# A decoder trunk on one core: all SBUF operands at one address modulo 256, another order of the first chunks, and a position read requested one unit earlier

## The chip, the cores and the metric

The kernel runs on one core of a Trainium2 chip. The metric is the device time of one execution in microseconds, shown as the median of several runs. Lower is better. A profiled execution has its own time and a span, which is the time from its first to its last instruction. TensorE is called PE below (PEld is its load of the stationary operand), VectorE is DVE, ScalarE is ACT, GpSimd is POOL, and SyncE is SP.

## The reference

One layer works on 1024 positions of 1024 float32 values each. In short:

```python
hn = rms_norm(h)
proj = hn @ w_in                                   # 1024 x 10256: u, v, lru, ssd, dt and gate columns
ya = u * (tril(w_s) @ layer_norm(gelu(v)) + b_s)   # position mixing in chunks of 128, 8 groups
yb = gelu(gate) * linear_scan(conv(xb))            # RG-LRU, 8 heads
yc = ssd(conv(xbc), dt, z)                         # Mamba-2 chunked scan, 4 groups
h = h + (sum_k sigmoid(g_k) * (y_k @ w_branch_k)) @ w_out
h = h + relu(rms_norm(h) @ w_up) ** 2 @ w_down
out = rms_norm(h)
```

The large products are made in three fp32r passes each (high times high, high times low, low times high), so every float32 operand is first split into a high and a low part: ACT writes the high part and DVE or POOL the difference. The two products of the last block use Strassen's seven products on half matrices.

## The kernel before

The code is one function, `trunk_kernel`. Its stages follow each other in this order:

- **The first chunks** (0 to about 58 us, lines 283 to 419), written out by hand, each engine in program order. The eight row chunks of `x` (128 positions each) are squared and summed on ACT (`row_sum`, line 319), their reciprocal root is made by `row_root` (line 322: for row 0 wholly on DVE, for the others three DVE and twelve POOL operations), they are scaled (`row_scale`, lines 325 to 328: on DVE or, with `True`, on POOL), transposed on PE (`transpose_rows`, line 159) and split (`x_high` on ACT, `x_low` on DVE). `v_start` makes the first block of v from them, 24 matmuls for each chunk. 18 matmuls of `ones` by `ones` (line 338, `WARM`) run first, while the first loads are under way. The norm's gains come from the DMA of line 294 through a transpose (line 344) and a copy to `g2c` (line 345).
- **Constants** (lines 421 to 453): transposes of the position weights `wT` (line 443), and the row sums of `wT` by a float32 matmul with `ones` (line 450), which feed `bs`. From here on a planner puts the instructions in order by priority; matmuls wait in PE's program order.
- **The other blocks of v** (`v_block`), with a layer norm of v whose result is written to DRAM as `vn_d` (line 825).
- **Units** (`run`, line 494): each unit is a product of 48 matmuls (line 492, `ps <- w . X`) with a `post` that takes its result. Three units' weights are prepared ahead. After each unit, `step` advances every generator in `pending` by one `yield`. `dt_stages` (line 526) is such a generator: softplus and `adt` in the first step, then, one unit later, matmuls with `tri` and `ones` (lines 534 and 535). `gmlp_unit` (line 765) is another: its first step requests the group's slice of `vn_d` on POOL's queue (line 768), the second, one unit later, multiplies it by `wT` (line 774).
- **The branches** (the second `run`): the same product, with the mixers' outputs `Y` in place of `X`; then `w_out` (line 917).
- **Up and down** (line 948, `seventh`), and the last norm (lines 1364 to 1425), whose reciprocal roots are in tiles `rs0` to `rs7`.

**Where operands lie.** Pools are stacked in SBUF in the order in which they are opened; `xn` and `act3` are taken from the other end. A tile of the small pool takes at least 32 bytes. The allocation of this kernel, in bytes of each partition:

| pool | names in the profile | first address | tile, bytes | address modulo 256 |
|---|---|---|---|---|
| base | ident, g2c, vh | 16512 | | 128, 128, 224 |
| w | wh, wl, wb, wt | 17632 | 4096 | 224 |
| raw | raw, rt | 42208 | 4096 | 224 |
| small | rsq, rs, fs, ... | 50400 | | |
| half | h | 51808 | 2048 | 96 |
| act | a | 84576 | 4096 | 96 |
| act2, opened where half was | a | 51808 | 4096 | 96 |
| lru | lr, lw | 146016 | 1024 | 96 |
| const | bs, wT, ones, tri, ... | 149088 | | bs, wT, ones: 0 |
| xn and act3 | xn, b | 163808 | 4096 | 224 |

Slices of these tiles that are operands of fp32r matmuls begin at multiples of 512 bytes from the tile's start, so an operand has its pool's residue. Right after the small pool come the pools half, act and const, whose start its size sets. The small pool begins with a tile that nothing uses:

```python
    sm(8, "spacer")
```

Of the kernel before, what the change touches and what calls it, by code (L numbers as in the profile page):

```python
# [9 lines left out]
F32R = mybir.dt.float32r  # L10
# [6 lines left out]
P = 128  # L17
# [10 lines left out]
C_U, C_V, C_XB, C_GATE, C_Z, C_XBC, C_DT, C_G = 0, 1024, 2048, 3072, 4096, 5120, 7168, 7184  # L28

VBLOCKS = ((678, 346, False), (0, 340, True), (340, 338, False))  # L30
WARM = 18
AHEAD = 2

# [2 lines left out]
def trunk_kernel(ctx: ExitStack, tc: tile.TileContext, x, norm_mix_g, w_in, b_gate, gmlp_ln_g, gmlp_ln_b,  # L36
# [42 lines left out]
    def sm(n, tag, dt=F32, bufs=None):  # L79
        return small.tile([P, n], dt, tag=tag, name=nm(tag), bufs=bufs)  # L80

    sm(8, "spacer")

    tt = nc.vector.tensor_tensor
    stt = nc.vector.scalar_tensor_tensor
# [197 lines left out]
    with tc.manual_schedule():  # L283

        rows, v_ps, xt = [], [None] * NCH, [None] * NCH

        def row_load(c):
            rows.append(act())
            nc.sync.dma_start(out=rows[c], in_=x[c * P:(c + 1) * P, :])

        g_rows = act()[:16, :P]
        row_load(0)
        for i, g in enumerate((norm_mix_g, norm_mlp_g)):
            nc.scalar.dma_start(out=g_rows[8 * i:8 * i + 8, :], in_=g[0].rearrange("(n p) -> n p", p=P))
        v_raw[0][0] = v_load(0, 0, rawp)
        row_load(1)
        v_raw[0][1] = v_load(0, 1, rawp)
        for i in (2, 3):
            v_raw[0][i] = v_load(0, i, None)
        for c in range(2, NCH):  # L300
            row_load(c)

        ident = base.tile([P, P], F32, name="ident")
        make_identity(nc, ident)
        ones = const.tile([P, P], F32, name="ones")
        nc.vector.memset(ones, 1.0)
        tri = const.tile([P, P], F32, name="tri")
        nc.gpsimd.affine_select(out=tri, in_=ones, pattern=[[1, P]], compare_op=ALU.is_ge, fill=0.0,
                                base=0, channel_multiplier=-1)
        neg = const.tile([P, P], F32, name="neg")  # L310
        ts(out=neg, in0=tri, scalar1=-1.0, scalar2=3.0e38, op0=ALU.add, op1=ALU.mult)
        g2c = base.tile([P, 2 * KD], F32, name="g2c")
        eps4 = base.tile([P, 1], F32, name="eps4")
        nc.vector.memset(eps4, 4.0 * EPS)
        ss, rs = sm(NCH, "ss"), sm(NCH, "rsx")
        v2[NCH - 1] = act()

        def row_sum(c):
            actv(v2[NCH - 1], rows[c], AF.Square, accum_out=ss[:, c:c + 1])

        def row_root(a, b):
            (rsqrt_cols if a else rsqrt_col)(rs[:, a:b], ss[:, a:b], 1.0 / D, EPS)

        def row_scale(c, pool=False):
            if pool:
                nc.gpsimd.tensor_scalar(out=rows[c], in0=rows[c], scalar1=rs[:, c:c + 1], scalar2=0.0, op0=ALU.mult, op1=ALU.add)
            else:
                ts(out=rows[c], in0=rows[c], scalar1=rs[:, c:c + 1], scalar2=None, op0=ALU.mult)

        def v_start(c, ks):  # L330
            if ks[0] == 0:
                v_ps[c] = aux()
            v_matmuls(0, wv0, c, v_ps[c], ks)


        ps = aux()
        for i in range(WARM):
            mm(ps[:, :P], ones, ones, start=True, stop=True)
        row_sum(0)
        row_root(0, 1)  # L340
        row_scale(0)
        wv0 = v_weights(0, (0,), nc.gpsimd)
        ps = aux()
        nc.tensor.transpose(out=ps[:, :16], in_=g_rows[:16, :], identity=ident[:16, :16])
        actv(g2c, ps[:, :16], AF.Copy)
        xt[0] = transpose_rows(rows[0])
        row_sum(1)
        row_root(1, 2)
        wv0 += v_weights(0, (1,))
        x_high(xt[0], 0, 0)  # L350
        x_low(xt[0], 0, 0)
        x_high(xt[0], 0, 1)
        row_scale(1)
        x_low(xt[0], 0, 1)
        v_start(0, range(0, 4))
        xt[1] = transpose_rows(rows[1])
        wv0 += v_weights(0, (2,), nc.gpsimd, nc.vector)
        wv0 += v_weights(0, (3,), None, nc.vector)
        v_start(0, range(4, 8))
        row_sum(2)  # L360
        row_root(2, 3)
        for q in range(2):
            x_high(xt[1], 1, q)
            x_low(xt[1], 1, q)
        row_scale(2)
        row_sum(3)
        row_sum(4)
        row_root(3, 5)
        row_scale(3, True)
        row_scale(4, True)  # L370

        for i in range(2):
            v_raw[1][i] = v_load(1, i, rawp)
        nc.sync.dma_start(out=dtb, in_=ssd_dt_bias[0].partition_broadcast(P))
        load_rows(acs, [b_gate.rearrange("k (n p) -> (k n) p", p=P), rows_of(gmlp_ln_g[0]), rows_of(gmlp_ln_b[0]),
                        rows_of(lru_conv_b[0]), rows_of(lru_b_r[0]), rows_of(lru_b_i[0]), rows_of(lru_lambda[0]),
                        rows_of(ssd_norm_g[0]), rows_of(ssd_conv_b[0]),
                        lru_conv_w[0].rearrange("k (n p) -> (k n) p", p=P)])
        load_rows(nacs, [ssd_conv_w[0].rearrange("k (n p) -> (k n) p", p=P)])
        nc.sync.dma_start(out=wT, in_=gmlp_w_s[0].rearrange("g t s -> t g s"))  # L380
        nc.sync.dma_start(out=bs, in_=gmlp_b_s[0].partition_broadcast(P))
        nc.sync.dma_start(out=al, in_=ssd_a_log[0].partition_broadcast(P))
        v_start(1, range(0, 4))
        xt[2] = transpose_rows(rows[2])
        v_start(1, range(4, 8))
        wv1 = []
        for c in range(1, NCH):

            if c > 1:
                if c + 1 < NCH:  # L390
                    xt[c + 1] = transpose_rows(rows[c + 1])
                v_start(c, range(0, 8))
            sq = gelu_in(c - 1)
            if c + 1 < NCH:
                x_high(xt[c + 1], c + 1, 0)
                x_low(xt[c + 1], c + 1, 0)
            if v2[c - 1] is None:
                v2[c - 1] = act()
            gelu_out(c - 1, sq)
            if c + 1 < NCH:  # L400
                x_high(xt[c + 1], c + 1, 1)
                x_low(xt[c + 1], c + 1, 1)
            if c in (1, 2):
                for i in ((5,), (6, 7))[c - 1]:
                    row_sum(i)
            if c == 2:
                row_root(5, 8)
                for i in (5, 6, 7):
                    row_scale(i, True)
            if c == 4:  # L410
                nc.gpsimd.affine_select(out=wT, in_=wT, pattern=[[0, 8], [-1, P]], compare_op=ALU.is_ge, fill=0.0,
                                        base=0, channel_multiplier=1)
                nc.gpsimd.tensor_scalar(out=bs, in0=bs, scalar1=0.5, scalar2=0.0, op0=ALU.mult, op1=ALU.add)
                for h in range(2):
                    nc.sync.dma_start(out=dcol[64 * h:64 * h + 64, :], in_=ssd_d[0].rearrange("(t h) -> h t", h=2)[h].partition_broadcast(64))
            if c >= 4:
                wv1 += v_weights(1, (c - 4,), nc.gpsimd)
        gelu_out(NCH - 1, gelu_in(NCH - 1))
# [22 lines left out]
    wps = [aux() for _ in range(2)]  # L441
    for i in range(8):
        nc.tensor.transpose(out=wps[i // 4][:, i % 4 * P:(i % 4 + 1) * P], in_=wT[:, i, :], identity=ident)
    for q in range(2):
        actv(wT[:, q * 4:q * 4 + 4, :], wps[q].rearrange("p (c n) -> p c n", c=4), AF.Copy)


    for q in range(2):
        ps = aux()
        mm(ps, ones, wT[:, q * 4:q * 4 + 4, :].rearrange("p c n -> p (c n)"), start=True, stop=True)  # L450
        for i in range(4):
            g = q * 4 + i
            stt(out=bs[:, g, :], in0=ps[:, i * P:(i + 1) * P], scalar=vh[:, LNB + g:LNB + g + 1], in1=bs[:, g, :], op0=ALU.mult, op1=ALU.add)
# [72 lines left out]
    def dt_stages():  # L526
        softplus(dt.rearrange("p c h -> p (c h)"), dtr.rearrange("p c h -> p (c h)"))
        tc.keep_in_program_order(actv(na, al, AF.Exp))
        ts(out=adt, in0=dt, scalar1=-1.0, scalar2=None, op0=ALU.mult)
        tt(out=adt, in0=adt, in1=na.unsqueeze(1).to_broadcast([P, NCH, 16]), op=ALU.mult)  # L530
        yield
        adt_f = adt.rearrange("p c h -> p (c h)")
        ps_a = aux()
# [175 lines left out]
    def lru_units(h):  # L709
# [16 lines left out]
        def post_g(ps):  # L726
            S["g2"] = act()
            gelu2(S["g2"], ps, T)
            later(stages())

        def stages():
            xb, w = S["xb"], S["w"]
# [29 lines left out]
        unit_in(C_GATE + h * P, post_g)  # L762


    def gmlp_unit(g):
        def stages(u2):
            vg = act((P, NCH, P))
            nc.gpsimd.dma_start(out=vg, in_=vn_d[:, g * P:(g + 1) * P].rearrange("(c p) d -> p c d", p=P))
            yield
            y = act()  # L770
            for half in range(2):
                ps = aux()
# [7 lines left out]
        def post(ps):  # L780
            u2 = act()
            gelu2(u2, ps, T)
            later(stages(u2))

        unit_in(C_U + g * P, post)

# [438 lines left out]
    with tc.manual_schedule():  # L1225
# [126 lines left out]
        for c in (4, 5, 6, 7, 0, 1, 2, 3):  # L1352
            H[c] = act()
            nc.scalar.dma_start(out=H[c], in_=h_d[c])
            if c == 7:
                dn_product(0, 0)
                prev.p4()
                prev.last_sum()
        sums, scaled = {}, {}

        def out_row(c, nb, o):
            nc.sync.dma_start(out=out[c * P:(c + 1) * P, hsl(nb)], in_=o)

        def row_scale(c):
            rs = sm(1, f"rs{c}")
            tt(out=sums[c, 0], in0=sums[c, 0], in1=sums[c, 1], op=ALU.add)
            rsqrt_col(rs, sums[c, 0], 1.0 / D, EPS)
            return rs
# [75 lines left out]
```

## Time and profile before

| | us |
|---|---|
| median of 3 runs | 2046.13 (2044.41 to 2046.42) |
| the profiled execution | 2047.5 |
| its span | 2045.8 |
| PE busy | 2001.9 (98%) |
| DVE busy | 1197.6 (59%) |
| ACT busy | 786.3 (38%) |
| POOL busy | 349.8 (17%) |
| mean granted PE clock | 0.993 of full |

In the groups and the timeline a row names a line of the kernel, an engine, the tiles (out<-in, with the moving and the stationary operand for a matmul), and the count. A busy matmul is longer than the distance to the next one, because matmuls are pipelined; what counts is the distance from start to start. Times in a timeline are from the start of the span, and what stands in brackets is the idle time of the engine before the row and what ended it.

### The profile page before, as it was taken

How to read it: one execution, taken by the hardware profiler on the slowest of the kernel's cores; microseconds unless marked ns; L12 is line 12 of the kernel's file. 1: busy time of each engine (PE TensorE's matmuls, PEld its weight loads, DVE VectorE, ACT ScalarE, POOL GpSimd, SP SyncE). 2: the span in 40 equal slices, each digit the busy share in tenths (PEclk: the TensorE clock that was granted, in tenths of full speed). 3: DMA queues.
4: the chain of work that ended last, by engine and by line, in shares of the span. 5: the costliest groups of instructions: out<-in, count | busy, mean ns of one | idle time of the engine just before them, and what ended most of it. 6: DMA issues, size and time to landing. Idle time of an engine off the chain costs nothing.

```text
span 2045.8 us, 23749 instructions
## 1 busy us (share of the span) xinstructions
PE 2001.9 (98%) x9300; PEld 1658.2 (81%) x9300; DVE 1197.6 (59%) x1822; ACT 786.3 (38%) x1076; POOL 349.8 (17%) x374
## 2 busy tenths in 40 slices
PE   8999999999999999999999999999899999999996
PEld 7988888888888888888888888887788887888885
DVE  6596864784585668431122224336756557787687
ACT  6422542353244325322221111146555555243243
POOL 5102232223124113332000320000111110000000
PEclk9999999999999999999999999999999999999998
DMA  4324233423333323343333442421443448544532
GB/s 155 81 108 88 76 95 82 97 72 95 74 85 100 75 78 93 113 124 114 103 103 109 147 125 83 155 82 63 165 160 125 168 149 300 189 135 133 185 105 92
DMA packets 202213, 239.39 MB, mean 117 GB/s; under 512 B 11140, under 2 KB 148564, under 8 KB 202100
## 3 DMA queue, kind: packets, MB, share of 16 engines
q1 hardware_dynamic: 175636, 144.91, 24.0%
q0 software_dynamic: 21680, 75.64, 11.3%
q10 hardware_dynamic: 4784, 17.31, 2.4%
q8 instruction: 73, 1.20, 0.2%
q14 instruction: 40, 0.33, 0.1%
HBM read 174.78 MB, written 63.05 MB: 116 GB/s over the span
## 4 chain that ended last, share of the span: by engine, by line
PE 83%; DVE 8%; ACT 4%; issue 2%; POOL 2%; DMA 1%; ACTq 0%; POOLq 0%; DVEq 0%
PE ps L492 47%; PE aux L948 26%; PE aux L917 4%; PE aux L255 2%; PE aux L740 1%; PE aux L774 1%; DVE rsq_q L109 1%; PE aux L639 1%; PE aux L659 1%; ACT a L977 1%; PE aux L663 1%; DVE bst L819 0%; PE aux L677 0%; ACT a L130 0%; DVE b L131 0%
## 5 line engine op out<-in xcount | busy, mean ns | idle before, releaser
L492 PE MATMUL ps<-xn,wh 128*128 128x512 f32 x2304 | 625.1, 392 | 0.0
L492 PEld LDWEIGHTS ps<-xn,wh 128*128 128x128 f32 x2304 | 431.0, 188 | 93.1 <-issue 4.2
L492 PE MATMUL ps<-xn,wl 128*128 128x512 f32 x1152 | 354.9, 389 | 0.0
L130 ACT ACTIVATE wh<-raw 128x1024 fp32r<-128x1024 f32 x96 | 101.7, 1059 | 402.9 <-PE ps L492 327.1
L492 PEld LDWEIGHTS ps<-xn,wl 128*128 128x128 f32 x1152 | 216.3, 188 | 45.5
L948 PE MATMUL aux<-a,b 128*128 128x512 f32 x864 | 203.0, 395 | 0.0
L948 PEld LDWEIGHTS aux<-a,b 128*128 128x128 f32 x864 | 162.2, 188 | 39.2
L131 DVE TENSOR_TENSOR wl<-raw,wh 128x1024 fp32r<-128x1024 f32 x64 | 81.4, 1272 | 180.7 <-ACT wh L130 180.5
L131 POOL TENSOR_TENSOR wl<-raw,wh 128x1024 fp32r<-128x1024 f32 x32 | 76.8, 2400 | 557.2 <-ACT wh L130 530.6
L948 PE MATMUL aux<-b,wt 128*128 128x512 f32 x672 | 157.2, 389 | 0.0
L948 PEld LDWEIGHTS aux<-b,wt 128*128 128x128 f32 x672 | 126.2, 188 | 26.6
L492 PE MATMUL ps<-a,wh 128*128 128x512 f32 x512 | 140.3, 395 | 0.0
L492 PEld LDWEIGHTS ps<-a,wh 128*128 128x128 f32 x512 | 96.1, 188 | 23.3
L948 PE MATMUL aux<-b,b 128*128 128x512 f32 x480 | 110.8, 389 | 0.0
L1197 DVE TENSOR_TENSOR a<-aux,a 128x512 f32<-128x512 f32 x112 | 77.0, 688 | 55.8 <-PE aux L948 55.7
L948 PEld LDWEIGHTS aux<-b,b 128*128 128x128 f32 x480 | 90.1, 188 | 19.0
L130 ACT ACTIVATE b<-wt 128x1024 fp32r<-128x1024 f32 x60 | 61.8, 1053 | 73.3 <-DMA wt<-u_d 61.5
L948 PE MATMUL aux<-a,wt 128*128 128x512 f32 x336 | 82.3, 401 | 3.3 <-ACT a L1074 3.3
L492 PE MATMUL ps<-a,wl 128*128 128x512 f32 x256 | 80.6, 395 | 0.0
L948 PEld LDWEIGHTS aux<-a,wt 128*128 128x128 f32 x336 | 64.1, 191 | 19.4 <-ACT a L1074 4.2
L512 DVE SCALAR_TENSOR_TENSOR a<-ps,scw,a 128x1023 f32<-128x1023 f32 (+2 forms) x48 | 61.4, 1280 | 25.6 <-ACT a L510 24.5
L1049 POOL DMA_DIRECT2D u_d<-a x48 | 34.5, 720 | 228.6 <-DVE a L1097 177.5
(292 smaller groups left out, 2951.5 us busy)
## 6 DMA issues: line engine op xcount, KB each, us to landing
raw<-in_w_in_dram SPq DMA_DIRECT2D x72, 512.0 KB
wt<-u_d SPq DMA_DIRECT2D x54, 512.0 KB
u_d<-a POOLq DMA_DIRECT2D x48, 512.0 KB, 4.9
rt<-in_w_mlp_up_dram SPq DMA_DIRECT2D x17, 512.0 KB
a<-acs_d POOLq DMA_DIRECT2D x32, 256.0 KB, 6.9
g_d<-a POOLq DMA_DIRECT2D x16, 512.0 KB, 5.2
a<-g_d ACTq DMA_DIRECT2D x16, 512.0 KB
a<-in_w_mlp_down_dram SPq DMA_DIRECT2D x16, 512.0 KB
```

What stands on the lines that cost most here:

```text
L109: stt(out=q, in0=r, scalar=nh, in1=r, op0=ALU.mult, op1=ALU.mult)
L130: actv(dst_hi, src, AF.Copy)
L131: (eng or nc.vector).tensor_tensor(out=dst_lo, in0=src, in1=dst_hi.bitcast(F32), op=ALU.subtract)
L255: mm(ps[:, :nt], X.tok(a, k, c), wk[k][w], start=(k == 0 and i == 0), stop=(k == KD - 1 and i == 2))
L492: mm(ps[:, hsl(h)], w[wi][:, k, :], a.rhs(ai, k, h), start=(n == 0), stop=(n == 3 * KD - 1))
L512: stt(out=dst[:, j:], in0=ps[:, :T - j], scalar=taps[3 - j], in1=dst[:, j:], op0=ALU.mult, op1=ALU.add)
L639: mm(st[:, cc * 256:cc * 256 + 256], Bt[:, 2 * q + cc, :], xw[q][:, cc].rearrange("p h d -> p (h d)"), start=True, stop=True)
L659: mm(yo[:, tok(i)], pv[c // 2][:, c % 2, j * P:(j + 1) * P], Cf[:, tok(c)], start=True, stop=True)
L917: mm(ps, M.tok(a, k, c), wo[nb][k][w], start=(k == 0 and a + w == 0), stop=(k == KD - 1 and a == 1))
L948: mm(ps, lhs[l][kk], rhs[r][kk], start=(new and n == 0), stop=(n == 11), skip_group_check=not new)
L1049: nc.gpsimd.dma_start(out=u_d[i:i + 2, self.s].rearrange("f p t -> p f t"), in_=t.rearrange("p (f t) -> p f t", f=2))
L1197: tt(out=h, in0=ps, in1=h, op=ALU.add)
```

## The change

- The unused first tile of the small pool grows from 8 to 32 floats (96 bytes more), and the eight tiles `rs0` to `rs7` (32 bytes each) become columns of one tile `roots` (32 bytes), 224 less. The pool gets 128 bytes smaller, and every pool after it moves down by 128: half, act, act2 and lru from residue 96 to 224, const from 0 to 128.
- In the first chunks the transpose to `g2c` is put between the ninth and the tenth warm-up matmul, and its copy ahead of `row_sum(0)` on ACT. The high part of the third weight pair is made by ACT in place of DVE. The root of row 2 alone and that of rows 3 and 4 become one root of rows 2 to 4; sums of rows 5 to 7 are spread differently.
- The row sums of `wT` are made by two fp32r matmuls on a split copy, in place of a float32 matmul.
- `dt_stages` waits one unit more before its matmuls.
- The slice of `vn_d` for group g+1 is requested in the `post` of group g, that for group 0 in the `post` of the last RG-LRU gate.

```diff
+SPACER = 32
-    sm(8, "spacer")
+    sm(SPACER, "spacer")
...
-        ps = aux()
+        ps, gps = aux(), aux()
         for i in range(WARM):
+            if i == WARM // 2:
+                nc.tensor.transpose(out=gps[:, :16], in_=g_rows[:16, :], identity=ident[:16, :16])
             mm(ps[:, :P], ones, ones, start=True, stop=True)
+        actv(g2c, gps[:, :16], AF.Copy)
         row_sum(0)
         row_root(0, 1)
         row_scale(0)
         wv0 = v_weights(0, (0,), nc.gpsimd)
-        ps = aux()
-        nc.tensor.transpose(out=ps[:, :16], in_=g_rows[:16, :], identity=ident[:16, :16])
-        actv(g2c, ps[:, :16], AF.Copy)
         xt[0] = transpose_rows(rows[0])
...
-        wv0 += v_weights(0, (2,), nc.gpsimd, nc.vector)
+        wv0 += v_weights(0, (2,), nc.gpsimd)
         wv0 += v_weights(0, (3,), None, nc.vector)
         v_start(0, range(4, 8))
         row_sum(2)
-        row_root(2, 3)
-        for q in range(2):
-            x_high(xt[1], 1, q)
-            x_low(xt[1], 1, q)
-        row_scale(2)
+        x_high(xt[1], 1, 0)
+        x_high(xt[1], 1, 1)
         row_sum(3)
         row_sum(4)
-        row_root(3, 5)
+        x_low(xt[1], 1, 0)
+        row_root(2, 5)
+        x_low(xt[1], 1, 1)
+        row_scale(2)
         row_scale(3, True)
         row_scale(4, True)
+        row_sum(5)
...
             if c in (1, 2):
-                for i in ((5,), (6, 7))[c - 1]:
-                    row_sum(i)
+                row_sum(c + 5)
...
+    wsum, one_r = [act((P, 2, HF), F32R) for _ in range(2)], act(dt=F32R)[:, :P]
+    actv(one_r, ones, AF.Copy)
     for q in range(2):
+        split(wsum[q][:, 0], wsum[q][:, 1], wps[q])
         actv(wT[:, q * 4:q * 4 + 4, :], wps[q].rearrange("p (c n) -> p c n", c=4), AF.Copy)
...
-        mm(ps, ones, wT[:, q * 4:q * 4 + 4, :].rearrange("p c n -> p (c n)"), start=True, stop=True)
+        for i in range(2):
+            mm(ps, one_r, wsum[q][:, i], start=(i == 0), stop=(i == 1))
...
         tt(out=adt, in0=adt, in1=na.unsqueeze(1).to_broadcast([P, NCH, 16]), op=ALU.mult)
+        yield
         yield
...
             later(stages())
+            if h == 7:
+                v_group(0)
...
+    v_of = {}
+
+    def v_group(g):
+        if g < 8:
+            v_of[g] = act((P, NCH, P))
+            nc.gpsimd.dma_start(out=v_of[g], in_=vn_d[:, g * P:(g + 1) * P].rearrange("(c p) d -> p c d", p=P))
+
     def gmlp_unit(g):
         def stages(u2):
-            vg = act((P, NCH, P))
-            nc.gpsimd.dma_start(out=vg, in_=vn_d[:, g * P:(g + 1) * P].rearrange("(c p) d -> p c d", p=P))
             yield
+            vg = v_of.pop(g)
...
             later(stages(u2))
+            v_group(g + 1)
...
+        roots = sm(NCH, "roots")
...
-            rs = sm(1, f"rs{c}")
+            rs = roots[:, c:c + 1]
```

## The prediction

> **What bounds the kernel now.** I read the page's busy times first, then who waited for whom on PE.
>
> ```profile
> PE 2001.9 (98%) x9300; PEld 1658.2 (81%) x9300; DVE 1197.6 (59%) x1822; ACT 786.3 (38%) x1076; POOL 349.8 (17%) x374
> ...
> PE rps L159 <- POOL a L326: 3.2, 2, 2.1
> PE rps L159 <- DVE a L328: 3.0, 3, 1.2
> PE aux L774 <- DMA a<-vn_d: 2.4, 1, 2.4
> PE aux L534 <- DVE adt L530: 0.9, 1, 0.9
> ```
>
> The columns of the waits are total, times and longest, in us. PE is busy for 98% of the span and has few waits, so time is gained where the distance between two matmuls shrinks or where one of these waits goes. The distance is read from PE's timeline, from one row's start to the next, divided by the count.
>
> ```profile
> 1025.74 1.07 PE L492 MATMUL ps<-xn,wh 128*128 128x512 f32 x4
> 1027.10 1.09 PE L492 MATMUL ps<-a,wh 128*128 128x512 f32 x4
> 1028.49 1.10 PE L492 MATMUL ps<-a,wh 128*128 128x512 f32 x4
> 1504.92 2.89 PE L948 MATMUL aux<-a,a 128*128 128x512 f32 x12
> 1507.65 8.33 PE L948 MATMUL aux<-b,wt 128*128 128x512 f32 x36
> 1796.12 22.55 PE L948 MATMUL aux<-a,b 128*128 128x512 f32 x96
> 1818.51 11.06 PE L948 MATMUL aux<-b,b 128*128 128x512 f32 x48
> 1829.41 0.86 PE L948 MATMUL aux<-a,b 128*128 128x512 f32 x3
> ```
>
> All are fp32r matmuls of 512 columns at the full clock. From 1796.12 to 1818.51 lie 96 matmuls of a with b: 22.39 / 96 = 233.2 ns each. The 48 of b with b take 10.90 / 48 = 227.1; the 12 of a with a take 2.73 / 12 = 227.5. The six from 1025.74 (four with wh, two with wl, xn moving) take 1.36 / 6 = 226.7; the six from 1027.10, with a moving, 1.39 / 6 = 231.7. By the table of addresses a lies at residue 96, and b, xn, wh, wl and wt at 224. So pairs of one residue take 227, whether both are at 96 or both at 224; pairs of different residues take about 6 ns more. Neither the engine load around them nor the tile's own address sorts the rows like that.
>
> **The change part by part.**
>
> **Addresses.** The small pool loses 128 bytes, and a goes from 96 to 96 - 128 = 224 modulo 256. These are the groups whose residues differ now and will be equal, by line and form:
>
> ```profile
> L948 PE MATMUL aux<-a,b 128*128 128x512 f32 x864 | 203.0, 395 | 0.0
> L492 PE MATMUL ps<-a,wh 128*128 128x512 f32 x512 | 140.3, 395 | 0.0
> L948 PE MATMUL aux<-a,wt 128*128 128x512 f32 x336 | 82.3, 401 | 3.3 <-ACT a L1074 3.3
> L492 PE MATMUL ps<-a,wl 128*128 128x512 f32 x256 | 80.6, 395 | 0.0
> L917 PE MATMUL aux<-a,b 128*128 128x512 f32 x240 | 59.5, 401 | 0.0
> L1219 PE MATMUL aux<-a,wt 128*128 128x512 f32 x48 | 13.2, 438 | 2.0 <-ACT a L130 1.2 <-DVE a L131 0.8
> L948 PE MATMUL aux<-b,a 128*128 128x512 f32 x48 | 11.6, 396 | 0.0
> ```
>
> Their count is 864 + 512 + 336 + 256 + 240 + 48 + 48 = 2304. At 233.2 - 227.1 = 6.1 ns that is 14.1 us. Not all reaches the end. The last two groups (96 matmuls, 0.6) lie ahead of the wait of line 1219, where ACT and DVE are late. And from here on DVE sets the end:
>
> ```profile
> 2010.03 0.69 DVE L1197 TENSOR_TENSOR a<-aux,a 128x512 f32<-128x512 f32 x1 [2.11 <-PE aux L948]
> ```
>
> This is DVE's last idle before the norm's tail. The block of 96 a with b that is then running ends at 2018.23, so 8.2 / 0.233 = 35 matmuls (0.2 us) come too late to help. I take 14.1 - 0.8 = 13.3. The bounds are 0 (the residue is not the cause) and 14.1. The small tile roots brings no wait: DVE writes one column per row, and ACT's reads of the column before it have ended in the tail by then.
>
> The v blocks are narrower, and there h with xn and a with xn differ now:
>
> ```profile
> 65.78 3.04 PE L255 MATMUL aux<-wb,xn 128*128 128x356 f32 x18
> 68.66 1.13 PE L255 MATMUL aux<-a,xn 128*128 128x356 f32 x6
> 99.78 19.53 PE L255 MATMUL aux<-h,xn 128*128 128x338 f32 x121
> ```
>
> With 356 columns an equal pair takes 2.88 / 18 = 160.0 and an unequal one (1.13 - 0.32) / 5 = 162, the last matmul's 0.32 left off. With 338 columns the unequal ones take (19.53 - 0.32) / 120 = 160; what an equal one takes no row shows: at least 160 - 18 * 227 / 512 = 152, if it goes by columns. There are 8 chunks * 24 = 192 of 346, 192 of 338 and 48 of 356 columns, 432 in all. The bounds are 0 and 432 * 8 = 3.5 us; by the nearest row, 1.7 ns or so, I take 0.7.
>
> [...]
>
> **Position values.**
>
> ```profile
> 830.79 1.80 POOL L768 DMA_DIRECT2D a<-vn_d  x2
> 836.70 3.58 PE L774 MATMUL aux<-wT,a 128*128 128x128 f32 x16 [2.42 <-DMA a<-vn_d]
> 836.60:840.00 3.40, 3.31 (x15) 3.34 (x16) 2.28 (x3) 1.06 (x1) 0.00 (x0) 0.50 0.62 176
> ```
>
> The last is a row of the view by windows; 0.50 is the granted clock. The first request on POOL stands at 830.79, behind the last RG-LRU head's work, and two slices are requested together; PE waits 2.42 for the first. In the change it is issued in the post of the last gate, ahead of that head's work, a unit (48 * 0.227 + stages, 12 us) earlier; 836.7 - 830.8 = 5.9 us are needed. The next slice stays behind the head's work, at about 830, but is needed a unit later. So the wait goes: 2.4. After it the clock was halved for 3.40 us, so 1.7 us of work were lost; no idle, no halving: 1.7 more. Sum 4.1, bounds 0 (the request is held by another wait) and 4.1. The extra tile of a is taken when the last SSD group has released its own.
>
> [...]
>
> **Dt.** The matmul of line 534 waits 0.9 for softplus; a unit later, after 12 us, adt is long there, and its readers start two units on. Gain 0.9, bounds 0 and 1.0.
>
> **First chunks.**
>
> ```profile
> 1.12 7.13 PE L338 MATMUL aux<-ones 128*128 128x128 f32 x36 [1.12 <-DVE ones L306]
> 4.51 1.06 ACT L319 ACTIVATE a<-a 128x1024 f32<-128x1024 f32 x1 [1.49 <-DMA a<-in_x_dram]
> 8.45 0.18 ACT L345 ACTIVATE g2c<-aux 128x16 f32<-128x16 f32 x1 [1.37 <-PE aux L344]
> 19.07 0.15 DVE L116 TENSOR_SCALAR rsqn_r<-ss 128x1 f32<-128x1 f32 x1
> 19.64 0.18 ACT L319 ACTIVATION_READ_ACCUMULATOR a<-a 128x1 f32 x1
> 22.96 0.75 DVE L328 TENSOR_SCALAR a<-a,rsx 128x1024 f32<-128x1024 f32 x1 [1.30 <-POOL rsx L124]
> 23.77 1.09 PE L159 MATMUL rps<-ident,a 128*128 128x128 f32 x8 [0.84 <-DVE a L328]
> 28.85 1.09 PE L159 MATMUL rps<-ident,a 128*128 128x128 f32 x8 [2.08 <-POOL a L326]
> 39.59 1.09 PE L159 MATMUL rps<-ident,a 128*128 128x128 f32 x8 [1.13 <-POOL a L326]
> ```
>
> The transpose to g2c comes at half of the warm-up, 1.12 + 7.13 / 2 = 4.7; ACT's copy follows at about 5.0 and ends at 5.2. It stands ahead of row_sum(0), which started at 4.51, so row 0's chain starts 0.7 later. ACT's high part in place of DVE's frees POOL's low part earlier and takes a short PE stall away, but then one root for rows 2 to 4 waits for the sums of rows 3 and 4: these ended at 19.82, now 0.7 later at 20.5. The root and the scaling take 23.71 - 19.07 = 4.6, so row 2's transposes go from 23.77 to about 25.3, with PE idle for some 4 us and the clock likely halved after it. In return rows 3 and 4 are scaled at once: row 3's transposes come when row 2's chunk is through, 3.0 later, at 28.3 to 29.5 instead of 28.85. Before row 5's root one sum fewer (1.06 + 0.19) stands on ACT, which covers the 1.13 at 39.59. I take a gain of 0.5 in all. Bounds: gain 4.8 (the waits of 0.84, 2.08 and 1.13 all go, with 0.7 of halved clock), loss 2 (the 0.7, and 1.3 of clock and late transposes).
>
> **Row sums of wT.**
>
> ```profile
> 60.11 1.98 PE L450 MATMUL aux<-wT,ones 128*128 128x512 f32 x4
> 61.52 3.45 PE L255 MATMUL aux<-wb,xn 128*128 128x356 f32 x18
> ```
>
> Four fp32r matmuls at 227 are 0.9 in place of 61.52 - 60.11 = 1.4. But they wait for a split, on DVE 0.69 for 512 columns as in line 1197, twice, and ACT has two more copies. I take a loss of 0.3, bounds gain 0.5 and loss 1.5.
>
> **Sum.** 13.3 + 0.7 + 4.1 + 0.9 + 0.5 - 0.3 = 19.2. The profiled execution took 2047.5, so 2028.3; it lies 1.4 above the median of 2046.13, against which the forecast is 2027.
>
> **The rivals.**
>
> - *Addresses do nothing.* What sorts the rows would be something else that goes with them, and 14.0 of the sum fall away: 2046.1 - 5.2 = 2041. Against it stand rows of 227 in one stage and for one line with rows of 233.
> - *The gain is eaten in the last product.* DVE is nearest its limit there, and PE would wait for split operands. From 1796 to 2010 and in the block before it lie most of the 864 a with b; if all of these gain nothing, 864 * 6.1 = 5.3 are lost: 2032. Against it: PE has no wait in that stage and DVE idles 2.11 at its end.
> - *The request stays late.* If the slot for slice 0, or POOL's queue, holds it, 4.1 stay: 2031.
> - *Slower: one address for all.* When everything shares a residue, ACT's, DVE's and POOL's accesses to a meet PE's reads of xn and wh, and no pair is fast. Its place is the units:
>
> ```profile
> L492 PE MATMUL ps<-xn,wh 128*128 128x512 f32 x2304 | 625.1, 392 | 0.0
> L492 PE MATMUL ps<-xn,wl 128*128 128x512 f32 x1152 | 354.9, 389 | 0.0
> ```
>
> If these 3456 take 6.1 more and the 2304 stay at 233, the time is 2041 + 21 = 2062. It decides from 5.1 / 3456 = 1.5 ns on. Against it: a with a, where DVE works on a too, and b with b take 227.
>
> **How the numbers follow.** Forecast 76%, addresses nothing 8%, eaten 7%, request late 5%, slower 4%. What a measurement tells from no change is 0.2%, 4.1 us: below 2042.0 is faster. Forecast, eaten, late and most of the second case lie below it: 0.93; no change 0.03; slower 0.04. The forecast's own range takes the narrow v blocks (2.8 better), the first chunks (4.3 better, 2.5 worse), the wT sums (0.8 better, 1.2 worse) and one clock halving more or fewer (1.7): 2019 to 2033. With the two rivals beside it I give 2018 to 2036.
>
> **What would show it.** Rows of a with b and a with wh at 227; no wait on vn_d, no 0.50 near 836; no wait at line 534; row 2's transposes later, rows 3 and 5 without a wait. Rows at 233 with equal residues would make it wrong.

## The result and the profile after

| | before | after |
|---|---|---|
| median, us | 2046.22 (2044.41 to 2046.51) | 2031.64 (2030.49 to 2033.04) |
| the profiled execution | 2047.5 | 2033.04 |
| its span | 2045.8 | 2031.3 |
| mean granted PE clock | 0.993 | 0.991 |

After over before is 0.9931, with a 95% interval of 0.9918 to 0.9944: 14.6 us faster. The forecast was 2027, so the change gained 4.6 less than forecast, while the time lies within the range.

The first lines are from the page of the kernel after: its busy times, and, from its groups by line and form, three that the prediction listed (busy time, mean ns of one). Lines have moved: the unit product is now line 497, `seventh` line 963, the last subtraction line 1212.

```profile
PE 1985.2 (98%) x9300; PEld 1658.2 (82%) x9300; DVE 1196.5 (59%) x1819; ACT 788.4 (39%) x1081; POOL 348.7 (17%) x362
...
L963 PE MATMUL aux<-a,b 128*128 128x512 f32 x864 | 197.3, 389 | 0.0
...
L497 PE MATMUL ps<-a,wh 128*128 128x512 f32 x512 | 136.8, 389 | 0.0
...
L963 PE MATMUL aux<-a,wt 128*128 128x512 f32 x336 | 80.3, 396 | 3.4 <-ACT a L1089 3.4
```

PE has the same 9300 matmuls and is 16.7 us less busy. Each of these three groups, whose residues became equal, lost 5 to 6 ns in the mean (395 to 389, 395 to 389, 401 to 396). The distance from start to start says the same, in PE's timeline of the kernel after:

```profile
1785.48 21.92 PE L963 MATMUL aux<-a,b 128*128 128x512 f32 x96
1807.24 11.04 PE L963 MATMUL aux<-b,b 128*128 128x512 f32 x48
1818.12 12.18 PE L963 MATMUL aux<-a,b 128*128 128x512 f32 x53
```

96 of a with b take 21.76 us, 226.7 ns each, where they took 233.2; the 48 of b with b take 10.88 / 48 = 226.7. Six with a moving (four with wh, two with wl) take 1.36 from 1025.97 on, 226.7 each, where they took 1.39 before.

To see where the rest went, I compare when the same matmul starts in the two traces:

| from, to | before, us | after, us | gained (+) or lost (-) |
|---|---|---|---|
| start of the span to the last matmul of the first v block | 57.34 | 58.56 | -1.2 |
| to the first of the second v block | 4.18 | 5.46 | -1.3 |
| to the last of the second v block | 31.07 | 32.49 | -1.4 |
| to the first unit | 30.87 | 30.86 | 0.0 |
| first unit to the 53rd | 662.82 | 662.27 | +0.6 |
| to the 61st (position values requested) | 104.61 | 100.27 | +4.3 |
| to the first of w_out (branches) | 402.45 | 397.18 | +5.3 |
| to the first of up and down | 110.65 | 109.79 | +0.9 |
| to the last matmul | 624.91 | 616.85 | +8.1 |
| to the end of the span | 16.89 | 17.60 | -0.7 |

The last three stages of matmuls (5.3, 0.9 and 8.1) hold the addresses' gain. The request gained 4.3. The start lost 3.9, where the prediction had a gain of 0.9 (chunks 0.5, narrow v blocks 0.7, row sums -0.3). The waits of PE after, and its clock in three windows, show the start (columns of the windows: length, busy times of PE, PEld, DVE, ACT and POOL, granted clock, DMA share, GB/s):

```profile
PE rps L160 <- DVE a L329: 6.2, 2, 4.8
...
PE rps L160 <- DVE rsqn_r L117: 2.5, 1, 2.5
...
PE aux L455 <- ACT a L131: 1.2, 1, 1.2
...
PE aux L549 <- DVE w L546: 1.0, 1, 1.0
...
23.90:30.70 6.80, 4.30 (x17) 4.30 (x18) 3.14 (x9) 3.14 (x10) 3.94 (x8) 0.50 0.54 160
64.80:68.20 3.40, 3.40 (x14) 3.40 (x13) 3.40 (x18) 0.53 (x2) 0.00 (x0) 0.51 0.00 0
836.60:840.00 3.40, 3.40 (x25) 3.11 (x24) 1.68 (x2) 1.97 (x2) 0.00 (x0) 1.00 0.91 228
```

The waits on vn_d and on adt are gone from the list. New in it are a wait of 2.5 for row 0 (1.22 before), one of 4.8 for row 2 and one of 1.2 for the split of the wT sums, and the wait for adt came back at line 549 as one for `w` of line 546. The clock is no longer halved at 836.6 (1.00, before 0.50), but it is from 23.9 on for 6.8 us (0.50; before, one stretch of 3.4 at 0.50 from 17.4 on) and at 64.8 (0.51), where the kernel before had full clock (1.00).

### The profile page after: what moved, and what is told of

It is laid out like the page before. It is cut to its first block, busy times and chain, and to the rows that moved or that the text cites. A ratio compares the mean times of both kernels' runs of the same rounds, so it can differ in the third digit from the quotient of the medians.

```text
span 2031.3 us, 23733 instructions
## 1 busy us (share of the span) xinstructions
PE 1985.2 (98%) x9300; PEld 1658.2 (82%) x9300; DVE 1196.5 (59%) x1819; ACT 788.4 (39%) x1081; POOL 348.7 (17%) x362
## 4 chain that ended last, share of the span: by engine, by line
PE 87%; DVE 5%; ACT 4%; issue 2%; POOL 1%; ACTq 0%; POOLq 0%; DVEq 0%
PE ps L497 49%; PE aux L963 26%; PE aux L256 4%; PE aux L932 3%; PE aux L748 1%; ACT a L992 1%; PE aux L788 1%; PE aux L645 1%; DVE rsq_q L110 1%; PE aux L665 1%; PE aux L669 1%; PE aux L683 0%; ACT a L131 0%; DVE b L132 0%; ACT a L970 0%
## 5 line engine op out<-in xcount | busy, mean ns | idle before, releaser
L963 PE MATMUL aux<-a,b 128*128 128x512 f32 x864 | 197.3, 389 | 0.0
```

Of the source, the lines that this page charges most:

```text
L963: mm(ps, lhs[l][kk], rhs[r][kk], start=(new and n == 0), stop=(n == 11), skip_group_check=not new)
```

## The experiments

The theory after the result: equal residues give 14 us and the request gives 4; the chunks, the wT sums and dt give nothing or lose. The rivals, tested against it: that something else than the residue makes the matmuls faster; that only the distance of 128 is slow; that the start's losses are one loss, in the chunks.

### Addresses alone

```diff
 (on the kernel before)
-    sm(8, "spacer")
+    sm(32, "spacer")
...
+        roots = sm(NCH, "roots")
...
-            rs = sm(1, f"rs{c}")
+            rs = roots[:, c:c + 1]
```

> The kernel before with the change of addresses alone: the unused first tile grows to 32 floats and the eight one-column tiles become columns of one tile, so that a lies at residue 224. The theory (the residue of a matmul's two operands sets the distance to the next) expects all fp32r matmuls of 512 columns at 227 ns and 13.3 us less than before, about 2033 us, with the waits on vn_d and at the dt matmul still there. The rival (what sorts the rows is something else) expects 233 ns for a with b as before and about 2046 us.

Measured: 2031.36 (2029.8 to 2033.41), ratio 0.9932 (0.992 to 0.9944), 14.3 us under the kernel before. PE's waits and timeline:

```profile
PE aux L774 <- DMA a<-vn_d: 2.2, 1, 2.2
...
1784.54 21.92 PE L948 MATMUL aux<-a,b 128*128 128x512 f32 x96
1806.30 11.04 PE L948 MATMUL aux<-b,b 128*128 128x512 f32 x48
```

The wait on vn_d is still there, and a with b takes 21.76 / 96 = 226.7. So the 128 bytes alone are worth what the whole change is worth. The remaining four parts together are worth nothing that these runs can tell.

### Other residues

```diff
 (on the kernel after, three kernels)
-SPACER = 32
+SPACER = 64     # a at 96, distance 128
+SPACER = 16     # a at 160, distance 64
+SPACER = 24     # a at 192, distance 32
```

> The changed kernel with an unused tile of 64 floats, so that a is back at residue 96, a distance of 128 from w and b, and all else is as changed. The theory expects 233 ns for a with b and a with wh, 227 for the rest, and 13 us more than the changed kernel, about 2045 us. The rival expects the changed kernel's 2031.6 us.

> The changed kernel with an unused tile of 16 floats: a at residue 160, a distance of 64 from w and b. No theory of mine has a sharp number for this distance: if any difference costs the same, 233 ns and about 2045 us; if the cost goes with the distance, about 230 ns and 2038 us; if only a distance of 128 costs, 227 ns and 2031.6 us.

> The changed kernel with an unused tile of 24 floats: a at residue 192, a distance of 32 from w and b. If any difference costs the same, 233 ns and about 2045 us; if the cost goes with the distance, about 228.5 ns and 2035 us; if only a distance of 128 costs, 227 ns and 2031.6 us.

Measured: 2047.67 (2045.8 to 2049.11), 2048.19 (2046.51 to 2050.02) and 2048.33 (2047.51 to 2049.73); ratios 1.001 (1.0001 to 1.0019), 1.0013 (1.0004 to 1.0022) and 1.0014 (1.0005 to 1.0023). PE's timeline for distance 64, then for distance 32:

```profile
1797.37 22.56 PE L963 MATMUL aux<-a,b 128*128 128x512 f32 x96
1819.77 10.61 PE L963 MATMUL aux<-b,b 128*128 128x512 f32 x46
```

```profile
1796.86 22.56 PE L963 MATMUL aux<-a,b 128*128 128x512 f32 x96
1819.27 11.07 PE L963 MATMUL aux<-b,b 128*128 128x512 f32 x48
```

22.40 / 96 = 233.3 and 22.41 / 96 = 233.4. At distance 128 the 96 take 22.39 from 1797.26 on, 233.2 each. At these three distances the price is the same; of these kernels only those with equal residues have a with b at 226.7. These three also show the rest of the change without its addresses: 2.0 to 2.6 us slower than the kernel before, by the medians (that of before was 2045.7 beside them). So undoing the addresses in the kernel after costs 16.0 to 16.7, where alone they gained 14.3 on the kernel before; what makes the 2 us between was not tried.

### The first chunks

Three kernels: the old order, the copy to `g2c` late, and the root of row 2 alone.

```diff
 (old order of the first chunks: all edits of that part undone)
...
 (g2c late)
-        actv(g2c, gps[:, :16], AF.Copy)
         row_sum(0)
...
         wv0 = v_weights(0, (0,), nc.gpsimd)
+        actv(g2c, gps[:, :16], AF.Copy)
...
 (root alone)
         row_sum(2)
+        row_root(2, 3)
         x_high(xt[1], 1, 0)
...
         x_low(xt[1], 1, 0)
-        row_root(2, 5)
-        x_low(xt[1], 1, 1)
         row_scale(2)
+        row_root(3, 5)
+        x_low(xt[1], 1, 1)
```

> The changed kernel with the order of the first chunks as before. The ledger from the two profiles (row 0's transposes 1.3 us later, row 2's 2.6, the end of the first block 1.2) expects the block's end at 57.4 and 1.2 us less than the changed kernel, about 2030.4 us. The rival, the prediction's term, expects 0.5 us more than the changed kernel, about 2032.1 us.

> The changed kernel with the copy to g2c behind row_sum(0) and the first weights on ACT; its transpose stays within the warm-up. If the copy's place holds row 0 back, row 0's transposes come 1.3 us earlier, at 9.6, and those of row 2 as much earlier, at 25.1; the time is about 2030.7 us. If POOL's work beside DVE's root sets row 0, they stay near 10.9 and the time stays 2031.6 us.

> The changed kernel with the root of row 2 by itself right after its sum, and one root for rows 3 and 4. If the common root holds row 2 back, its transposes come at about 22 in place of 26.4, PE's wait of 4.8 us goes to below 1.5, the clock is not halved for 6.8 us there, and the time is about 2029.5 us. If rows 3 and 4 are then as late as in the kernel before, the gain goes to a wait at row 3: about 2031 us.

Measured: 2030.34 (2029.62 to 2031.59), ratio 0.9924 (0.991 to 0.9937), with the old order; 2030.06 (2028.83 to 2031.31), 0.9922 (0.9905 to 0.9938), with g2c late; 2029.36 (2028.57 to 2031.2), 0.9919 (0.9905 to 0.9934), with the root alone. The intervals overlap that of the kernel after, so the sizes are taken from the place itself. First the kernel after, from the warm-up to row 3:

```profile
1.12 4.21 PE L341 MATMUL aux<-ones 128*128 128x128 f32 x18 [1.12 <-DVE ones L307]
5.42 0.26 PE L340 MATMUL aux<-ident,a 16*128 16x16 f32 x1
5.71 0.18 ACT L342 ACTIVATE g2c<-aux 128x16 f32<-128x16 f32 x1 [2.69 <-PE aux L340]
5.79 1.05 ACT L320 ACTIVATE a<-a 128x1024 f32<-128x1024 f32 x1
10.95 1.10 PE L160 MATMUL rps<-ident,a 128*128 128x128 f32 x8 [2.51 <-DVE rsqn_r L117]
21.60 0.17 DVE L117 TENSOR_SCALAR rsqn_r<-ss 128x3 f32<-128x3 f32 x1 [1.50 <-ACT a L320]
26.40 1.97 PE L160 MATMUL rps<-ident,a 128*128 128x128 f32 x8 [4.79 <-DVE a L329]
31.22 1.04 PE L160 MATMUL rps<-ident,a 128*128 128x128 f32 x8
```

Row 0's sum starts at 5.79 in place of 4.51, 1.28 later, and its transposes come 1.31 later (10.95, before 9.64): the whole delay is ACT standing behind the copy. The root of rows 2 to 4 starts at 21.60, and 4.8 later row 2's transposes start. Row 3 comes without a wait, and so does row 5: no wait of the transposes on POOL is left in the list of PE's waits. Row 0 and row 2 with g2c late:

```profile
9.62 1.09 PE L160 MATMUL rps<-ident,a 128*128 128x128 f32 x8 [1.89 <-DVE rsqn_r L117]
...
25.04 1.97 PE L160 MATMUL rps<-ident,a 128*128 128x128 f32 x8 [4.76 <-DVE a L329]
```

Row 0 has its 1.3 back, and row 2 stands 1.36 earlier with the same wait: two separate costs. Row 2 and row 3 with the root alone:

```profile
23.53 1.59 PE L160 MATMUL rps<-ident,a 128*128 128x128 f32 x8 [2.02 <-DVE a L329]
28.61 1.09 PE L160 MATMUL rps<-ident,a 128*128 128x128 f32 x8 [0.50 <-POOL a L327]
```

The wait for row 2 falls from 4.79 to 2.02, and what row 3 pays for it is 0.50. The last matmul of the first v block starts at 58.56 after, at 57.47 with the old order, at 56.70 with g2c late and at 55.99 with the root alone.

### The row sums of wT

```diff
 (on the kernel after)
-    wsum, one_r = [act((P, 2, HF), F32R) for _ in range(2)], act(dt=F32R)[:, :P]
-    actv(one_r, ones, AF.Copy)
...
-        split(wsum[q][:, 0], wsum[q][:, 1], wps[q])
...
-        for i in range(2):
-            mm(ps, one_r, wsum[q][:, i], start=(i == 0), stop=(i == 1))
+        mm(ps, ones, wT[:, q * 4:q * 4 + 4, :].rearrange("p c n -> p (c n)"), start=True, stop=True)
```

> The changed kernel with the row sums of wT by one float32 matmul each, as before. The ledger expects the 1.2 us in which PE waits for the split to go, and with it the halved clock at 64.8: 1.3 to 2.7 us less than the changed kernel, about 2029.5 us. The rival, the prediction's term, expects 0.3 us less, about 2031.3 us.

Measured: 2029.93 (2028.6 to 2032.42), ratio 0.9922 (0.991 to 0.9935). PE and ACT in the kernel after:

```profile
60.74 0.65 PE L444 MATMUL aux<-ident,wT 128*128 128x128 f32 x4 [0.96 <-DVE va L207]
61.67 0.29 ACT L446 ACTIVATE a<-ones 128x128 fp32r<-128x128 f32 x1
61.97 1.07 ACT L131 ACTIVATE a<-aux 128x512 fp32r<-128x512 f32 x2
62.60 1.23 PE L455 MATMUL aux<-a,a 128*128 128x512 f32 x3 [1.20 <-ACT a L131]
64.02 0.43 PE L256 MATMUL aux<-wb,xn 128*128 128x356 f32 x1 [0.19 <-ACT wT L449]
```

With the float32 sums, and the window that was at half clock:

```profile
61.24 0.65 PE L444 MATMUL aux<-ident,wT 128*128 128x128 f32 x4 [1.06 <-DVE va L207]
...
63.14 3.45 PE L256 MATMUL aux<-wb,xn 128*128 128x356 f32 x18
...
64.80:68.20 3.40, 3.40 (x24) 3.40 (x23) 3.40 (x18) 1.01 (x3) 0.00 (x0) 1.00 0.03 7
```

From the second group of wT's transposes to the second v block it takes 64.02 - 60.74 = 3.28 after, and 63.14 - 61.24 = 1.90 with the float32 sums. The new sums wait for ACT, which first copies `ones` and then the high parts, and the v block waits for ACT's copy of wT behind these. And PE's idle there (0.96, 1.20 and 0.19 within 4 us) is followed by a window at 0.51; without the 1.20 it is at 1.00. One pair of profiles could be chance; but with the new sums the 17 matmuls of wb with xn that follow take 4.48 in the kernel after, 3.71 with the old order, 4.17 with g2c late and 4.08 with the root alone, while 18 of them take 3.45 in the kernel before, here, and in the second kernel under "Together", all with float32 sums. So this part lost 1.3 to 1.4, and 1.4 of clock behind it.

### The transposes of dt

```diff
 (on the kernel after)
-        nc.tensor.transpose(out=ps_a[:, 2 * P:3 * P], in_=acs, identity=ident)
+        ps_t = aux()
+        nc.tensor.transpose(out=ps_t[:, :P], in_=acs, identity=ident)
...
```

> The changed kernel with the transpose of acs (line 549) in a PSUM tile of its own, so that it no longer has to follow the subtraction that reads the first tile (line 546), which stands behind a convolution step on DVE. If the wait removed at the dt matmul came back there, the 0.97 us at line 549 go: about 2030.7 us. If the wait is for acs itself, it stays: 2031.6 us.

Measured: 2030.93 (2030.25 to 2031.98), ratio 0.9927 (0.9913 to 0.994), which the runs can't tell from the kernel after. In the kernel after:

```profile
127.37 1.09 PE L497 MATMUL ps<-xn,wh 128*128 128x512 f32 x4
...
159.68 0.29 DVE L535 TENSOR_TENSOR adt<-adt,na 128x128 f32<-128x128 f32 x1
...
160.03 0.48 PE L540 MATMUL aux<-adt,tri 128*128 128x128 f32 x2
...
164.56 0.27 DVE L546 TENSOR_TENSOR w<-aux,acs 128x128 f32<-128x128 f32 x1
164.89 0.33 PE L549 MATMUL aux<-ident,acs 128*128 128x128 f32 x1 [0.97 <-DVE w L546]
```

With the transpose in a PSUM tile of its own:

```profile
159.85 0.49 PE L540 MATMUL aux<-adt,tri 128*128 128x128 f32 x2 [0.67 <-DVE adt L535]
161.10 0.27 PE L550 MATMUL aux<-ident,acs 128*128 128x128 f32 x1
```

The wait at the transpose is gone, and the transpose follows the 147th matmul of the units, where it followed the 158th. But the wait for adt is there again, 0.67. In the profiles with float32 sums, with the late request and with g2c late it is there too (1.07, 1.01 and 0.75), and there the transpose waits 0.04 at most though it shares its tile with the operand of line 546's subtraction. So the trace of the kernel after names that subtraction as what the transpose waited for, but this run alone doesn't show that the shared tile made the wait. In the twelve profiles with the extra step the two waits together are 0.7 to 1.1, in the two without it 0.9: the step moves the wait and doesn't remove it.

### The request in its own unit

```diff
 (on the kernel after)
             later(stages())
-            if h == 7:
-                v_group(0)
...
         def stages(u2):
+            v_group(g)
             yield
...
             later(stages(u2))
-            v_group(g + 1)
```

> The changed kernel with each slice of vn_d requested in its own unit, as before. The theory expects a wait on vn_d of about 2.4 us and a halved clock after it: 4.1 us more than the changed kernel, about 2035.7 us, the whole of it between the 52nd and the 60th unit. The rival (the wait is hidden by what else is late) expects 2031.6 us.

Measured: 2035.31 (2034.74 to 2037.0), ratio 0.9949 (0.9935 to 0.9963), 3.7 above the kernel after. Its timeline and the window behind the wait, and then the same place in the kernel after:

```profile
838.50 2.87 PE L787 MATMUL aux<-wT,a 128*128 128x128 f32 x16 [2.10 <-DMA a<-vn_d]
...
839.50:842.90 3.40, 3.40 (x15) 3.01 (x14) 2.34 (x3) 1.02 (x1) 0.00 (x0) 0.50 0.54 151
```

```profile
820.19 0.91 POOL L778 DMA_DIRECT2D a<-vn_d  x1
...
837.49 1.95 PE L788 MATMUL aux<-wT,a 128*128 128x128 f32 x16
```

2.10 of wait and 1.7 of halved clock come with the late request. The kernel before, with its late request, has a window at half clock behind its wait too (0.50 from 836.60), and the kernel after has 1.00 from 836.60 to 840.00. In the kernel after the first slice is requested 17.3 us ahead of its matmul.

### Together

Two kernels without the parts that lost: one with the old order of the chunks, the float32 sums and the transpose of dt in its own tile, and one with the new order instead, but g2c late and the root of row 2 alone.

> The addresses and the early request of the change, with the order of the first chunks and the row sums of wT as before, and the transpose of acs in a tile of its own. Addresses alone took 2031.4 us; the request is worth 4.0 and the wait at the dt matmuls 0.9: about 2026.5 us. If the halved clock comes back somewhere else, 2028 us.

> As the run before it, but with the changed order of the first chunks mended in two places: the copy to g2c behind row 0's work on ACT, and row 2's root by itself. If both mends work, row 2's transposes come at about 21 and row 5's without a wait: 1 to 2 us less than the run before it, about 2025 us. If not, 2026.5 us or more.

Measured: 2026.93 (2026.02 to 2027.3), ratio 0.9906 (0.9891 to 0.992), and 2024.81 (2023.61 to 2025.22), ratio 0.9895 (0.988 to 0.991). The second is 6.8 us under the kernel after, and faster than the kernel before and the kernel after. Its start:

```profile
9.63 1.09 PE L160 MATMUL rps<-ident,a 128*128 128x128 f32 x8 [1.87 <-DVE rsqn_r L117]
...
22.34 1.77 PE L160 MATMUL rps<-ident,a 128*128 128x128 f32 x8 [2.00 <-DVE a L329]
...
58.80 3.45 PE L256 MATMUL aux<-wb,xn 128*128 128x356 f32 x18
```

The last matmul of its first v block starts at 54.80, 2.5 earlier than before: the new order does pay once the copy and the common root are out of its way. The second v block starts at 58.80 where it started at 64.02 after and at 61.52 before. In its timeline that v block is 1.5 shorter than after, as in the kernel with float32 sums.

## Why the prediction was right, and where it was not

**Addresses: right, in mechanism and size.** Forecast 13.3; alone they measured 14.3, and the three late stages of the ledger hold 14.2 at the last matmul. Pairs of residues sorted all rows as read. The rivals that addresses do nothing (2041) and that one address makes all pairs slow (2062) fall with the rows at 226.7, for a with b and b with b alike. Four kernels that differ in one tile's size show 226.7 or 233.2 to 233.4 for a with b. The rival that the last product eats the gain (2032) gives nearly the measured time, but for a wrong reason: up and down gained 8.1, and 1248 matmuls there (a with b, a with wt and b with a) by the measured 233.2 - 226.7 = 6.5 ns are 8.1. The rival of the late request (2031) comes as near and falls as well: the request stands at 820.19, and no wait for it is left. By its time alone the run couldn't tell the forecast from these two; its rows do.

**The tail: 0.2 was forecast, 0.7 lost.** DVE's last idle before the norm ends at 1995.12:

```profile
1995.12 0.69 DVE L1212 TENSOR_TENSOR a<-aux,a 128x512 f32<-128x512 f32 x1 [2.03 <-PE aux L963]
2003.08 11.04 PE L963 MATMUL aux<-b,b 128*128 128x512 f32 x48
```

The a with b behind that point take 7.96 in place of 8.2, 0.24, as forecast. The rest is DVE's own chain: from there to the end of the span 36.2, before 2045.8 - 2010.03 = 35.8. What lengthened it by 0.4 was not tried; with the addresses alone the stretch from the last matmul to the end is 17.2, 0.3 longer than before.

**Position values: right.** Forecast 4.1, measured 4.3 in the trace and 3.7 by undoing it: the wait and the halved clock behind it went together.

**First chunks: a step that failed.** Forecast a gain of 0.5, measured a loss of 1.2, 1.1 against the old order. The prediction put the transpose to `g2c` "at half of the warm-up", 4.7, by dividing the whole warm-up's time by its count. The first half of it takes 4.21 and the second 2.84, so it came at 5.42 (4.91 to 5.65 in the nine other kernels that have it there); that made row 0 late by 1.3 in place of 0.7. From there the rest follows as worked out: the sums of rows 3 and 4 are done for the root at 21.60 (forecast 20.5), root and scaling take 4.8 (forecast 4.6), and row 2 comes at 26.40 (forecast 25.3). And the forecast of "likely halved" was priced inside a bound only; two windows, 6.8 us at 0.50, followed, where the kernel before had one of 3.4. That rows 3 and 5 come without a wait was right, and it was not enough. The trade itself was mis-sized: a root for three rows saved row 3's wait, which costs 0.50 with the root alone, for 2.8 on row 2.

**Row sums of wT: the sign was right, the size not.** Forecast a loss of 0.3, at most 1.5. I counted the time of the splits and named ACT's extra copies, but didn't follow ACT's order, in which a copy of `ones` and the high parts stand ahead of wT's copies, and I did not ask what PE's idle does to the clock. Measured 1.3 and 1.4, together more than the bound.

**Dt: a step that failed.** Forecast a gain of 0.9, "a unit later, after 12 us, adt is long there". It moved by five matmuls and not by 48: the matmul of line 540 starts 160.03 - 127.37 = 32.66 after the first unit, which is 144 * 0.2268, and before it followed the 139th, which starts at 154.76, 138 * 0.2268 after 123.46. DVE makes adt at the same place in both, 32.2 and 32.3 after the first unit, so it is no earlier against its reader. One more `yield` delays the reader in the order of the program, but here the planner's order kept it close to where it was; which priority did that was not tried. In the kernel after the wait then stood at the transpose of line 549, behind the reader of the same PSUM tile.

**Narrow v blocks.** Forecast 0.7, measured 0.0 in the ledger's last v block, and 0.1 in the second with the addresses alone (30.96 against 31.07). With 338 columns equal pairs take 160 too (below).

**The sum.** In the start to the first unit 4.8 less than forecast, and dt 0.9 less, in the tail 0.5 less; the units ahead of the request gave 0.6 (as they do with the addresses alone), the late matmuls 0.7 and the request 0.2 more. -4.8 - 0.9 - 0.5 + 0.6 + 0.7 + 0.2 = -4.7, against 4.6 by the medians. The forecast's own range began too high: its terms on the better side, 2.8, 4.3, 0.8 and 1.7, add up to 9.6, which gives 2017 and not 2019. The 1.7, for one halving more or fewer, has its size from the window at 836.6; that one comes or goes elsewhere was a guess. The runs showed the one at 836.6 gone, one more in the first chunks and one at 64.8, and the same place with and without a slower clock: behind row 0's wait the eight transposes take 1.10 in the kernel after (wait 2.51), and 1.97 with the float32 sums (wait 2.30), where the code up to there is the same. What "would show it": the rows at 227, no wait on vn_d, full clock near 836, rows 3 and 5 without a wait all hold. No wait at the reader of adt holds too, though it gained nothing, as it moved on to line 549.

## What to carry to other kernels

Where PE is busy all the time, sort its matmuls by where their two operands lie, and read the distance from start to start, before anything else is changed: moving the operands by 128 bytes was worth as much here as the whole change of five parts (14.3 against 14.6). Price an edit in the start by what it puts ahead of the first instruction on each engine. Ask of every PE idle of about 2 us, in one piece or in several close together, whether a window at half clock can follow, and allow for both answers: the wait of 2.08 for row 3 had none behind it in the kernel before (1.00 from 28.85 to 34.00), and with the root alone the wait of 2.02 for row 2, which ended at 23.53, lies in 14 us (20 to 34) with a mean clock of 0.88, which is 1.7 us lost. A reader that is delayed in the program text is late in the kernel only if the scheduler lets it be; look up where producer and reader stand against one fixed matmul.

## What the runs showed of the hardware

The cost of unequal residues was one step: 6.1 to 6.7 ns on 227 for distances of 32, 64 and 128 bytes alike (233.4, 233.3 and 233.2 against 226.7 to 227.1). By the table of addresses a, at 84448 in the kernel after, and wh, at 17632, differ by 261 times 256, and their pairs take 226.7 as those of a and b do, which differ by 310 times 256: these two multiples of 256 make no difference. Equal residues did not always give the same time: h and lw move together, and in the groups by line and form h with lw has a mean busy time of 397 ns at residue 224 (after and addresses alone), 399 at 96 (before) and 401 at 192. Why was not tried.

The step is seen with 512 columns. In the kernel after the v blocks have equal residues:

```profile
68.83 1.12 PE L256 MATMUL aux<-a,xn 128*128 128x356 f32 x6
69.79 3.04 PE L256 MATMUL aux<-wb,xn 128*128 128x356 f32 x18
...
96.67 13.58 PE L256 MATMUL aux<-h,xn 128*128 128x338 f32 x84
```

With 356 columns a with xn now takes 0.96 / 6 = 160, before 162; with 338 columns (13.58 - 0.32) / 83 = 160, as it took unequal. 338 and 356 columns take the same 160, so between these two the time of the matmuls is not set by their columns; unequal residues cost nothing at 338 and 2 ns at 356. What sets the 160, and why equal residues are faster, no run here shows.

From the first chunks to the last matmul the clock was halved for 3.40 us at a time in the profiles of both kernels (0.50 to 0.51; before from 17.4, 836.6, 1386.1, 1413.4 and 1457.8 on, after from 64.8, 1378.9, 1406.2 and 1450.6 on), or for twice 3.40 in one piece (after, from 23.9 on), and for no other length.
